# PLE operands as fp16 pairs split in the w_o stage, and DMA transposes for the last projection's x

## The chip, the cores and the metric

The kernel runs on one core of a Trainium2 chip. The metric is the device time of one execution in microseconds (us); lower is better. Engines are named as in the profile: PE (TensorE matmul), DVE (VectorE), ACT (ScalarE), POOL (GpSimd), SP (SyncE). "Full speed" of PE is its 2.4 GHz level, "half speed" its 1.2 GHz level.

## What is computed

One decoder layer on x of 1024 tokens by 1024 features, float32 in and out. Of the reference, cut to what matters here:

```
y  = sigmoid(gate_A) * (A @ W_A) + sigmoid(gate_B) * (Bm @ W_B);  x += y @ W_o
x += hierarchical MoE(RMSNorm(x))        # top-1 of 4 groups, then top-2 of 4 experts inside it
x += sigmoid(RMSNorm(x) @ W_pg) * (p @ W_ple)
```

p has 1024 tokens by 256 features, so `p @ W_ple` is a product of depth 256 (two slices of 128) and width 1024, called PLE below. `RMSNorm(x) @ W_pg` is the last projection: depth 1024, width 1024.

## The kernel before, in words

The tokens are cut in 8 tiles of 128. Products of float32 values are mostly done as three fp16 products: each operand is split into a high and a low fp16 part (`split`: ACT writes the high part, DVE the low part), and hi\*hi, lo\*hi and hi\*lo are summed in float32 in PSUM.

The program runs in stages:

- attention, convolution, gates and their merge, up to about 609 us;
- the **w_o stage**, about 609 to 697 us: for each token tile 48 matmuls of `out_proj`, then `norm2`, which writes fp16 high and low rows (`h2s`) and turns them by one DMA transpose on the SP queue (L682) for the router's small matmuls (`router_rows`, L688 and L690). The eight loads of x (L636) and the loads of `W_ple` (`wpl`) and of most of p transposed (`pTs`) go through the same SP queue;
- a **window**, about 697 to 724 us, in an order written out by hand on PE, ACT, DVE and POOL: the last third of the routing and the PLE products of token tiles 0 to 3, whose results are stored to memory. The routing ends in the table of token indices (`toki`, L985) from which POOL gathers the experts' rows (`xg`, `xtail`, L1010);
- 16 experts, about 720 to 964 us, whose weights arrive as 96 loads of 512 KB on the SP queue;
- six late PLE half tiles (`ple_late`), then a branch for overflow that all engines pass together (`tc.If`, L1254), and behind it the **final stage**, to the end: two more PLE half tiles, and for each token tile t its last projection.

In the final stage `combine` (with `mix`) gathers two rows per token by indirect DMAs from POOL (`yg`, L1239, four buffers) and adds them to `x2` on DVE (L1241); `turn` transposes x on PE (eight float32 transposes, L156, by `transpose_split`) and splits the result out of PSUM on ACT (L110) and DVE (L111); `final` does two half tiles of 24 matmuls (L1328 to L1330), and after each ACT applies the sigmoid (L1331), which frees the PSUM bank (there are two), and DVE multiplies by PLE and adds x (L1332, L1333). Each half tile's matmuls read the turned x of their own token tile. The PE order of the final stage is the order of the code; there `turn(t+1)` stands between the two halves of `final(t)`. ACT, DVE, POOL and SP are ordered by a scheduler.

`ple_mm` is the PLE product of one half tile: two float32 matmuls (the profile shows each as two rows of L889). A half tile in the final stage is evacuated by ACT in `ple_late` (L1234), one of the early ones in `evac` (L946).

Of the kernel before, what the change touches and what calls it, by code (L numbers as in the profile page):

```python
# [9 lines left out]
F32 = mybir.dt.float32  # L10
F32R = mybir.dt.float32r
BF = mybir.dt.bfloat16
FP16 = mybir.dt.float16
I32 = mybir.dt.int32
AF = mybir.ActivationFunctionType
# [4 lines left out]
S = 1024  # L20
D = 1024
NT = 8
# [12 lines left out]
NPL = 3  # L35
NPW = 4
# [11 lines left out]
XS = 16.0  # L48
# [3 lines left out]
HS = 256.0  # L52
PS = XS * HS
# [9 lines left out]
def trunk_layer(ctx: ExitStack, tc: tile.TileContext, x, wq0, wq, wc, wgb, wga, wA, wB, wo, wr,  # L63
                we, wpg, wple, pT, vecs, gains, out):
    nc = tc.nc
    def f(ap):
        return ap.bitcast(F32)

    def pool(stack, name, bufs=1, **kw):
        return stack.enter_context(tc.tile_pool(name=name, bufs=bufs, reuse_waits="tile", **kw))  # L70
# [37 lines left out]
    def split(hi, lo, src, lo_eng=None, scale=None):  # L108
        if scale is not None:
            nc.scalar.activation(hi, src, AF.Copy, scale=scale)  # L110
            nc.vector.scalar_tensor_tensor(lo, src, scale, hi, op0=ALU.mult, op1=ALU.subtract)  # L111
            return
        nc.scalar.activation(hi, src, AF.Copy)
        (lo_eng or nc.vector).tensor_tensor(lo, src, f(hi), op=ALU.subtract)
# [9 lines left out]
    def acc_bank():  # L124
        return bank("acc", 2)

    def tr_bank():
        return bank("tr", 2)
# [23 lines left out]
    def transpose_split(src, hi, lo, scale=None):  # L152
        for g in range(2):
            tr = tr_bank()
            for c in range(4):
                nc.tensor.transpose(tr[:, c * 128:(c + 1) * 128],  # L156
                                    src[:, (4 * g + c) * 128:(4 * g + c + 1) * 128], identF)
            t3 = tr.rearrange("p (c t) -> p c t", c=4)
            split(hi[:, 4 * g:4 * g + 4], lo[:, 4 * g:4 * g + 4], t3, scale=scale)
# [389 lines left out]
    def feat_mm(wp, h):  # L549
        acc = acc_bank()  # L550
        for k in range(8):
            mm3(acc, wp[0][:, k], wp[1][:, k], hTh[:, k, h * 512:(h + 1) * 512],
                hTl[:, k, h * 512:(h + 1) * 512], k, 8)
        return acc

    wBp = None
    for j in range(8):
# [4 lines left out]
        for h in range(2):  # L562
            hs = slice(h * 512, (h + 1) * 512)
            a = feat_mm(wb, h) if j else conv["b", h]
# [20 lines left out]
    wp_ = pool(mstack, "wo")  # L585
# [47 lines left out]
    x2 = xp.tile([128, NT, D], F32, name="x2")  # L633
# [1 line left out]
    for t in range(NT):  # L635
        nc.sync.dma_start(x2[:, t], x[t * 128:(t + 1) * 128, :])  # L636
    plep = pool(ctx, "ple", side="right")
    wpl = plep.tile([128, 2, D], F32, name="wpl")
    gp = pool(ctx, "route", side="right")
    rt = pool(ctx, "rt", side="right")  # L640
    pstack = ExitStack()
    plp0 = pool(pstack, "ple0", side="right")
    pTs = [pl_.tile([128, 2, n * 128], F32, name=f"pT{n}") for n, pl_ in ((NPL, plp0), (NT - NPL, plep))]
    fstack = ExitStack()
    fp = pool(fstack, "fw", side="right")
    gF = fp.tile([128, D], F32, name="gF")
# [14 lines left out]
    def out_proj(t, h, mid=None):  # L661
        tok = slice(t * 128, (t + 1) * 128)
        hs = slice(h * 512, (h + 1) * 512)
        a = acc_bank()
        for k in range(8):
            if k == 5 and mid:
                mid()
            wh, wl = wos[k]
            nc.tensor.matmul(a, lhsT=mTh[:, k, tok], rhs=wh[:, hs], start=k == 0, stop=False)
            nc.tensor.matmul(a, lhsT=mTl[:, k, tok], rhs=wh[:, hs], start=False, stop=False)  # L670
            nc.tensor.matmul(a, lhsT=mTh[:, k, tok], rhs=wl[:, hs], start=False, stop=k == 7)
        nc.vector.scalar_tensor_tensor(x2[:, t, hs], a, 1.0 / PS, x2[:, t, hs], op0=ALU.mult, op1=ALU.add)
# [12 lines left out]
    def router_rows(t, hT2):  # L685
        rb = o_bank()
        for k in range(8):
            nc.tensor.matmul(rb[:, :40], lhsT=hT2[:, 0, k], rhs=wrp[:, k].rearrange("p a e -> p (a e)"), start=k == 0,  # L688
                             stop=False)
            nc.tensor.matmul(rb[:, :20], lhsT=hT2[:, 1, k], rhs=wrp[:, k, 0], start=False, stop=k == 7)  # L690
        sm = fp.tile([128, 20], F32, name="sm", bufs=2)
        nc.vector.tensor_reduce(sm, rb[:, :40].rearrange("p (w e) -> p e w", e=20), axis=AX.X, op=ALU.add)
        nc.vector.scalar_tensor_tensor(lg[:, t], sm, 1.0 / PS, vt[:, 14:34], op0=ALU.mult, op1=ALU.add)
# [176 lines left out]
    for t in range(NT - 1):  # L870
        out_proj(t, 0)
        out_proj(t, 1)
        if t:
            router_rows(t - 1, hT2)
        hT2 = norm2(t)
        if t == 4:
            nc.sync.dma_start(wpl, wple)
            nc.sync.dma_start(pTs[0], pT[:, :, :NPL * 128])
            nc.sync.dma_start(pTs[1], pT[:, :, NPL * 128:])
        if t in CUTS[1:3]:  # L880
            i = CUTS.index(t)
            for _ in route(CUTS[i - 1], t, tb):
                pass

    def ple_mm(t, h, get=acc_bank):
        a = get()
        pTt, i = (pTs[0], t) if t < NPL else (pTs[1], t - NPL)
        for k in range(2):
            nc.tensor.matmul(a, lhsT=pTt[:, k, i * 128:(i + 1) * 128],  # L889
                             rhs=wpl[:, k, h * 512:(h + 1) * 512], start=k == 0, stop=k == 1)  # L890
        return a

    def ple_out(t, po):
        nc.scalar.dma_start(pl_d[t * 128:(t + 1) * 128, :], po)
# [37 lines left out]
    def ring_tile(name, i):  # L932
        return ring[0].tile([128, 1024], F32 if i == 1 else FP16, name=name, bufs=ring[i])
# [9 lines left out]
    po = [ring_tile("wraw", 1) for _ in range(NPW)]  # L943

    def evac(t, h, a):
        nc.scalar.activation(po[t][:, h * 512:(h + 1) * 512], a, AF.Copy)  # L946
        if h:
            ple_out(t, po[t])

# [21 lines left out]
    def w0_lo(i):  # L971
        gate_lo(w0[i])

    def ple_at(t, h, get):
        if t < NPL:
            evac(t, h, ple_mm(t, h, get))
# [14 lines left out]
    w0_lo(1)  # L991
    evac(3, 0, ple_mm(3, 0, s_bank))
    w0_lo(2)
    pstack.close()
    xstack = ExitStack()
    xq = pool(xstack, "moe", side="right")
    NB = (4, 2)
# [144 lines left out]
    for e, seq in enumerate(FIRST):  # L1142
        with tc.issue_after(mark.ins):
            halves, acts, nx = {}, [], None
            xT = xTs.pop(e)
            for c in seq:
                if c in "ABCD":
                    i = "ABCD".index(c)
# [3 lines left out]
                elif c == "h":  # L1152
                    we_, i = next(his)
                    gate_hi(allw[we_], we_src(we_))
                elif c == "l":
                    we_, i = next(lows)
# [14 lines left out]
    for e in range(e0, E - 1):  # L1171
# [3 lines left out]
        with ExitStack() as held:  # L1175
            if e < 3:
                held.enter_context(tc.issue_after(mark.ins))
            if e < E:
# [12 lines left out]
                xT, nx = xTs.pop(e), None  # L1191
# [20 lines left out]
    xT = xTs.pop(E - 1)  # L1212
# [3 lines left out]
    for c in LAST:  # L1216
        if c in "ABCD":
            i = "ABCD".index(c)
            halves[c] = expert_half(C, xT, ws, i // 2, i % 2)
        elif c == "k":  # L1220
            k = len(wps)
# [7 lines left out]
    pos = [ring_tile("wraw", 1) for _ in range(NPW, NT)]  # L1229

    def ple_late(i, get):
        t, h = NPW + i // 2, i % 2
        a = ple_mm(t, h, get)
        nc.scalar.activation(pos[t - NPW][:, h * 512:(h + 1) * 512], a, AF.Copy)  # L1234

    def mix(t, tile_):
        for c in range(2):
# [16 lines left out]
    with tc.If(ov > 0):  # L1254
# [12 lines left out]
        with tc.For_i(JB * E, 8 * E, E) as jb:  # L1267
            with tc.For_i(0, E) as ev:
# [6 lines left out]
                xT = expert_t(128, tl, xg)  # L1275
# [23 lines left out]
    ip = pool(ctx, "fin", side="right")  # L1299
# [11 lines left out]
        return plt  # L1311

    def turn(t):
        xh = ip.tile([128, 8, 128], FP16, name="xh", bufs=2)
        xl = ip.tile([128, 8, 128], FP16, name="xl", bufs=2)
        transpose_split(x2[:, t], xh, xl, 1.0)
        return xh, xl, row_norm(ip, x2[:, t], None, None, grow=HS)

    def final(t, plt, xh, xl, rs, mid):
        tok = slice(t * 128, (t + 1) * 128)  # L1320
        ot = ip.tile([128, D], F32, name="ot", bufs=3)
        edges = (0, 512, 1024) if t < NT - 1 else (0, 512, 768, 1024)
        for lo, hi in zip(edges, edges[1:]):
            hs = slice(lo, hi)
            a = acc_bank()[:, 0:hi - lo]
            for k in range(8):
                wh, wl = wps[k]
                nc.tensor.matmul(a, lhsT=xh[:, k], rhs=wh[:, hs], start=k == 0, stop=False)  # L1328
                nc.tensor.matmul(a, lhsT=xl[:, k], rhs=wh[:, hs], start=False, stop=False)  # L1329
                nc.tensor.matmul(a, lhsT=xh[:, k], rhs=wl[:, hs], start=False, stop=k == 7)  # L1330
            nc.scalar.activation(ot[:, hs], a, AF.Sigmoid, scale=rs)  # L1331
            V_.tensor_tensor(ot[:, hs], ot[:, hs], plt[:, hs], op=ALU.mult)  # L1332
            V_.tensor_tensor(ot[:, hs], ot[:, hs], x2[:, t, hs], op=ALU.add)  # L1333
            if t == NT - 1:
                nc.sync.dma_start(out[0, tok, hs], ot[:, hs])
            if lo == 0:
                nx = mid()
        if t < NT - 1:
            nc.scalar.dma_start(out[0, tok, :], ot)
        return nx  # L1340

    order.enter_context(tc.manual_schedule(engines={ET.PE}))
    with tc.high_priority():
        plts = [combine(0), combine(1)]
    for i in range(NQ, NR):
        ple_late(i, s_bank)
    with tc.high_priority():
        hs_ = turn(0)
    for i in range(NR, 2 * (NT - NPW)):
        ple_late(i, s_bank)  # L1350
    for t in range(NT):
        if t + 2 < NT:
            plts.append(combine(t + 2))
        hs_ = final(t, plts[t], *hs_, lambda: turn(t + 1) if t + 1 < NT else None)
    order.close()


# [77 lines left out]
```

## Time and profile before

| | before |
|---|---|
| median of 3 runs | 1088.74 us (1088.43 to 1091.41) |
| the profiled execution's own time | 1087.68 us |
| its span, first to last instruction | 1085.9 us |
| mean granted PE clock | 0.987 of full |
| busy PE / DVE / ACT / POOL | 1027.3 / 667.1 / 525.9 / 230.6 us |

The profiled execution takes 1.78 us more than its span, and stands 1.06 us below the median. Busy time of PE is read with care, since matmuls overlap: back to back, 128x512 fp16 matmuls start 0.2155 us apart although each row shows 0.38 us. The start times in the timeline give the pace. In the timelines the brackets hold the idle time ahead of an instruction and what ended it; queue entries that issue DMAs are marked SPq or ACTq.

### The profile page before, as it was taken

The numbers are of one execution on the slowest core, as the hardware profiler recorded it, in microseconds if no ns is written. First come the engines' busy times: TensorE is split into PE (matmuls) and PEld (weight loads), VectorE is DVE, ScalarE is ACT, GpSimd is POOL, SyncE is SP. The second block draws the span as 40 slices with busy tenths as digits, with TensorE's granted clock in tenths as the row PEclk, the third lists the DMA queues.
The fourth block names the chain that finished last, engine by engine and source line by source line (L and its number), as shares of the span: only waits on it lengthen the run. The fifth ranks groups of instructions, "written<-read, shape, count | busy, mean of one in ns | idle before, by whom it ended". The sixth has DMA issues, their size and how long they took to land. (4 is left out here: it accounts for less than half of the span.)

```text
span 1085.9 us, 17914 instructions
## 1 busy us (share of the span) xinstructions
PE 1027.3 (95%) x6664; PEld 589.9 (54%) x6664; DVE 667.1 (61%) x1430; ACT 525.9 (48%) x974; POOL 230.6 (21%) x343
## 2 busy tenths in 40 slices
PE   6898999999999999999998999887989999998898
PEld 4554555555555555444443444456767777744444
DVE  6778566676586572223248536748977888755643
ACT  6554455565555552212126322237767777553232
POOL 3552234223222100000015300231111110015300
PEclk9999999999999999999999999989999999998999
DMA  8257677568566763423448653399998999536501
GB/s 304 57 121 172 133 156 183 126 124 182 154 126 142 187 134 80 158 97 97 155 161 296 246 153 78 88 322 389 389 357 304 328 334 306 175 97 213 194 39 59
DMA packets 167117, 201.33 MB, mean 185 GB/s; under 512 B 122674, under 2 KB 126394, under 8 KB 166898
## 3 DMA queue, kind: packets, MB, share of 16 engines
q1 hardware_dynamic: 142898, 121.09, 39.9%
q0 software_dynamic: 15008, 53.29, 15.8%
q10 hardware_dynamic: 9120, 25.78, 6.5%
q8 instruction: 53, 0.87, 0.3%
q14 instruction: 38, 0.31, 0.1%
HBM read 138.69 MB, written 32.59 MB: 158 GB/s over the span
## 5 line engine op out<-in xcount | busy, mean ns | idle before, releaser
L117 PE MATMUL acc<-hTh,fwh 128*128 128x512 f16 x336 | 127.3, 379 | 1.3 <-DVE fg L419 1.1
L119 PE MATMUL acc<-hTh,fwl 128*128 128x512 f16 x336 | 127.3, 379 | 0.0
L118 PE MATMUL acc<-hTl,fwh 128*128 128x512 f16 x336 | 127.3, 379 | 0.0
L966 DVE SCALAR_TENSOR_TENSOR wl<-wraw,wh 128x1024 f16<-128x1024 f32 x64 | 77.9, 1220 | 22.6 <-ACT wh L961 21.7
L111 DVE SCALAR_TENSOR_TENSOR wl<-wraw,wh 128x1024 f16<-128x1024 f32 x47 | 57.9, 1245 | 51.0 <-ACT wh L110 48.9
L228 PE MATMUL acc<-wqh,hTh 128*128 128x384 f16 (+1 forms) x248 | 82.1, 331 | 5.1 <-ACT hTh L110 4.5
L229 PE MATMUL acc<-wqh,hTl 128*128 128x384 f16 (+1 forms) x248 | 82.3, 332 | 2.5 <-DVE hTl L111 2.5
L230 PE MATMUL acc<-wql,hTh 128*128 128x384 f16 (+1 forms) x248 | 82.4, 332 | 0.0
L314 ACT ACTIVATE P<-P,st 128x128 f32<-128x128 f32 (+3 forms) x64 | 49.5, 773 | 66.5 <-DVE st L311 51.1
L961 ACT ACTIVATE wh<-wraw 128x1024 f16<-128x1024 f32 x64 | 67.0, 1054 | 18.8 <-PE acc L1046 11.8
L110 ACT ACTIVATE wh<-wraw 128x1024 f16<-128x1024 f32 x47 | 49.1, 1055 | 54.2 <-PE acc L118 26.4
L323 DVE SCALAR_TENSOR_TENSOR hl<-P,st,hl 128x128 f16<-128x128 f32 (+3 forms) x64 | 52.7, 839 | 23.6 <-ACT hl L322 23.2
L306 DVE CUSTOM_DVE_ANT_0 P<-s,base 128x512 f32<-128x512 f32 (+2 forms) x96 | 51.6, 553 | 14.7 <-PE s L305 11.1
L1046 PEld LDWEIGHTS <-wh 128*128 128x128 f16 x512 | 50.5, 99 | 7.0 <-issue 3.4
L322 ACT ACTIVATE hl<-P,st 128x128 f16<-128x128 f32 (+3 forms) x64 | 46.7, 768 | 15.3 <-DMA pTr<-hl 8.6
L119 PEld LDWEIGHTS <-fwl 128*128 128x128 f16 x336 | 32.9, 98 | 37.8
L1329 PE MATMUL acc<-wh,xl 128*128 128x512 f16 (+1 forms) x136 | 50.2, 369 | 3.1 <-DVE xl L111 3.1
L1045 PEld LDWEIGHTS <-wh 128*128 128x128 f16 x512 | 51.1, 100 | 1.8
L118 PEld LDWEIGHTS <-fwh 128*128 128x128 f16 x336 | 32.9, 98 | 35.2 <-issue 1.7
L117 PEld LDWEIGHTS <-fwh 128*128 128x128 f16 x336 | 32.9, 98 | 34.2
L1328 PE MATMUL acc<-wh,xh 128*128 128x512 f16 (+1 forms) x136 | 50.4, 370 | 0.0
L1330 PE MATMUL acc<-wl,xh 128*128 128x512 f16 (+1 forms) x136 | 50.1, 368 | 0.0
(328 smaller groups left out, 2537.0 us busy)
## 6 DMA issues: line engine op xcount, KB each, us to landing
wraw<-in_we_dram SPq DMA_DIRECT2D x96, 512.0 KB
Yd<-yt ACTq DMA_DIRECT2D x14, 512.0 KB
fraw<-in_wc_dram POOLq DMA_DIRECT2D x12, 512.0 KB, 5.7
wraw<-in_wq_dram POOLq DMA_DIRECT2D x24, 192.0 KB, 4.0
P<-in_x_dram SPq DMA_DIRECT2D x8, 512.0 KB
fraw<-in_wga_dram POOLq DMA_DIRECT2D x8, 512.0 KB, 4.6
base<-brow POOLq DMA_DIRECT2D x8, 512.0 KB, 3.6
sga<-fg POOLq DMA_DIRECT2D x8, 512.0 KB, 3.4
```

What stands on the lines that cost most here:

```text
L111: nc.vector.scalar_tensor_tensor(lo, src, scale, hi, op0=ALU.mult, op1=ALU.subtract)
L117: nc.tensor.matmul(acc, lhsT=whi, rhs=xhi, start=k == 0, stop=False)
L118: nc.tensor.matmul(acc, lhsT=whi, rhs=xlo, start=False, stop=False)
L119: nc.tensor.matmul(acc, lhsT=wlo, rhs=xhi, start=False, stop=k == nk - 1)
L228: nc.tensor.matmul(acc[:, :w], lhsT=hTh[:, k, tok], rhs=wh[:, :w], start=k == 0, stop=False)
L229: nc.tensor.matmul(acc[:, :w], lhsT=hTl[:, k, tok], rhs=wh[:, :w], start=False, stop=False)
L230: nc.tensor.matmul(acc[:, :w], lhsT=hTh[:, k, tok], rhs=wl[:, :w], start=False, stop=k == 7)
L306: nc.vector.tensor_tensor_reduce(out=pt[:, c0:c0 + valid], in0=sb[:, :valid], in1=base[:, c0:c0 + valid], scale=1.0, scalar=-3e38, op0=ALU ...
L323: nc.vector.scalar_tensor_tensor(hl[:, :qt + 1, 1], p3, r, hl[:, :qt + 1, 0], op0=ALU.mult, op1=ALU.subtract)
L961: nc.scalar.activation(wh, raw, AF.Copy, scale=HS)
L966: V_.scalar_tensor_tensor(wl, raw, HS, wh, op0=ALU.mult, op1=ALU.subtract)
L1045: nc.tensor.matmul(a[:, :n], lhsT=wh[:, k], rhs=xT[:, k, 0, :n], start=k == 0, stop=False)
```

## The change

`W_ple` and p transposed are no longer loaded as float32 tiles. In the first four turns of the w_o stage's loop one 512 KB slice each (two of `wple`, then two of `pT`) is loaded through the single `woraw` buffer and split into fp16 pairs, and `ple_mm` does six fp16 matmuls in place of two float32 ones; the evacuations take the scale out. In the final stage tiles 0 and 1 are turned on PE as before, but both ahead of the last two PLE half tiles; tiles 2 to 7 are split in rows (token-major) into one `rows` buffer, and turned by a DMA transpose on the SP queue. `turn(t+2)` stands between the halves of `final(t)`. The turned x has three buffers, `ot` two.

```diff
-    wpl = plep.tile([128, 2, D], F32, name="wpl")
+    wpl = [plep.tile([128, 2, D], FP16, name=f"wpl{i}") for i in range(2)]
+    pTs = [plep.tile([128, 2, S], FP16, name=f"pT{i}") for i in range(2)]
...
-        if t == 4:
-            nc.sync.dma_start(wpl, wple)
-            nc.sync.dma_start(pTs[0], pT[:, :, :NPL * 128])
-            nc.sync.dma_start(pTs[1], pT[:, :, NPL * 128:])
+        if t < 4:
+            k = t % 2
+            dst, src, sc = ((wpl, wple, HS), (pTs, pT, XS))[t // 2]
+            raw = wp_.tile([128, D], F32, name="woraw", bufs=1)
+            nc.sync.dma_start(raw, src[:, k, :])
+            split(dst[0][:, k], dst[1][:, k], raw, scale=sc)
...
     def ple_mm(t, h, get=acc_bank):
         a = get()
-        pTt, i = (pTs[0], t) if t < NPL else (pTs[1], t - NPL)
+        tok, hs = slice(t * 128, (t + 1) * 128), slice(h * 512, (h + 1) * 512)
         for k in range(2):
-            nc.tensor.matmul(a, lhsT=pTt[:, k, i * 128:(i + 1) * 128],
-                             rhs=wpl[:, k, h * 512:(h + 1) * 512], start=k == 0, stop=k == 1)
+            nc.tensor.matmul(a, lhsT=pTs[0][:, k, tok], rhs=wpl[0][:, k, hs], start=k == 0, stop=False)
+            nc.tensor.matmul(a, lhsT=pTs[0][:, k, tok], rhs=wpl[1][:, k, hs], start=False, stop=False)
+            nc.tensor.matmul(a, lhsT=pTs[1][:, k, tok], rhs=wpl[0][:, k, hs], start=False, stop=k == 1)
         return a
...
     def turn(t):
-        xh = ip.tile([128, 8, 128], FP16, name="xh", bufs=2)
-        xl = ip.tile([128, 8, 128], FP16, name="xl", bufs=2)
-        transpose_split(x2[:, t], xh, xl, 1.0)
+        xT = ip.tile([128, 2, 8, 128], FP16, name="xT", bufs=3)
+        xh, xl = xT[:, 0], xT[:, 1]
+        if t < 2:
+            transpose_split(x2[:, t], xh, xl, 1.0)
+        else:
+            rows = ip.tile([128, 2, D], FP16, name="rows", bufs=1)
+            split(rows[:, 0], rows[:, 1], x2[:, t], scale=1.0)
+            nc.sync.dma_start_transpose(xT.rearrange("p a k t -> p (a k) t"), rows.rearrange("p a d -> p (a d)"))
         return xh, xl, row_norm(ip, x2[:, t], None, None, grow=HS)
...
-        ot = ip.tile([128, D], F32, name="ot", bufs=3)
+        ot = ip.tile([128, D], F32, name="ot", bufs=2)
...
-        hs_ = turn(0)
+        hs_ = [turn(0), turn(1)]
     for i in range(NR, 2 * (NT - NPW)):
         ple_late(i, s_bank)
     for t in range(NT):
         if t + 2 < NT:
             plts.append(combine(t + 2))
-        hs_ = final(t, plts[t], *hs_, lambda: turn(t + 1) if t + 1 < NT else None)
+        hs_ = [hs_[1], final(t, plts[t], *hs_[0], lambda: turn(t + 2) if t + 2 < NT else None)]
```

The change moves instructions in three places. First PE behind the branch (`tr<-identF,x` are the turns, `s<-wpl,pT` the last two PLE half tiles, `acc<-wh,xh` the last projection). Before:

```order
L1254 UNCONDITIONAL_BRANCH x2
L156 MATMUL tr<-identF,x_6008 128x128 x8
L889 MATMUL s<-wpl,pT_6032 128x512 x4
L1328 LDWEIGHTS xh
L1328 MATMUL acc<-wh,xh 128x512
L1329 LDWEIGHTS xl
L1329 MATMUL acc<-wh,xl 128x512
```

Now:

```order
L1254 UNCONDITIONAL_BRANCH x2
L156 MATMUL tr<-identF,x_6008 128x128 x16
L889 LDWEIGHTS pT_6023
L889 MATMUL s<-wpl_6021,pT_6023 128x512
L890 LDWEIGHTS pT_6023
L890 MATMUL s<-wpl_6022,pT_6023 128x512
L891 LDWEIGHTS pT_6024
L891 MATMUL s<-wpl_6021,pT_6024 128x512
```

The transposes of tile 1 now stand ahead of the PLE half tiles and of the whole of tile 0's projection; before they stood between its halves. Twelve PLE matmuls follow, then the last projection without any further transpose.

Second, ACT in the final stage (`s,rn_ss<-x` are the squares of the row norm, `xh<-tr` or `xT<-tr` the high parts of a turn on PE, `rows<-x` the high parts of a turn by DMA, `ot<-acc` the sigmoids, `wraw<-s` the PLE evacuations). Before:

```order
L140 ACTIVATE s,rn_ss<-x_6008 128x512 x2
L110 ACTIVATE xh<-tr 128x512 x2
L1234 ACTIVATE wraw<-s 128x512 x2
L140 ACTIVATE s,rn_ss<-x_6008 128x512 x2
L1331 ACTIVATE ot<-acc,rn_ss 128x512
L110 ACTIVATE xh<-tr 128x512 x2
L1331 ACTIVATE ot<-acc,rn_ss 128x512
L140 ACTIVATE s,rn_ss<-x_6008 128x512 x2
L1339 DMA out_dram<-ot 128x1024
L1331 ACTIVATE ot<-acc,rn_ss 128x512
```

Now, from the squares of tile 1:

```order
L140 ACTIVATE s,rn_ss<-x_6008 128x512 x2
L110 ACTIVATE xT<-tr 128x512 x2
L1234 ACTIVATE wraw<-s 128x512
L110 ACTIVATE rows<-x_6008 128x1024
L1234 ACTIVATE wraw<-s 128x512
L1336 ACTIVATE ot<-acc,rn_ss 128x512
L110 ACTIVATE rows<-x_6008 128x1024
L1336 ACTIVATE ot<-acc,rn_ss 128x512
L140 ACTIVATE s,rn_ss<-x_6008 128x512 x2
L110 ACTIVATE rows<-x_6008 128x1024
L1344 DMA out_dram<-ot 128x1024
L1336 ACTIVATE ot<-acc,rn_ss 128x512 x2
```

The row splits of tiles 2, 3 and 4 stand between the sigmoids of tile 0 and ahead of those of tile 1; each but the first waits until the transpose of the tile before has left the one `rows` buffer.

Third, the SP queue at the start of the w_o stage (`x` are the eight loads of x, `hT<-h2s` the DMA transposes of `norm2`). Before:

```order
L602 DMA g<-cgb 128x1024
L636 DMA x_6008<-in_x_dram 128x1024 x8
L877 DMA wpl<-in_wple_dram 128x2048
L879 DMA pT_6032<-in_pT_dram 128x2x640
L682 DMA_TRANSPOSE hT_6151<-h2s 128x16x128
L682 DMA_TRANSPOSE hT_6239<-h2s 128x16x128
```

Now:

```order
L602 DMA g<-cgb 128x1024
L636 DMA x_6008<-in_x_dram 128x1024 x8
L878 DMA woraw<-in_wple_dram 128x1024
L680 DMA_TRANSPOSE hT_6149<-h2s 128x16x128
L878 DMA woraw<-in_pT_dram 128x1024 x2
L680 DMA_TRANSPOSE hT_6241<-h2s 128x16x128
```

One of the four slices is loaded ahead of x; two now stand between the first and the second DMA transpose of `norm2`, and each waits until the split before it has read `woraw`.

## Rows read from the trace of the kernel before

**Rows 1.** Page, busy time by engine: busy us, share of the span, instructions.

```profile
PE 1027.3 (95%) x6664; PEld 589.9 (54%) x6664; DVE 667.1 (61%) x1430; ACT 525.9 (48%) x974; POOL 230.6 (21%) x343
```

**Rows 2.** Waits of PE, 960 to 1086 us, for a split: total, times, longest.

```profile
PE acc L1329 <- DVE xl L111: 3.1, 1, 3.1
```

**Rows 3.** Timeline of PE, late PLE and final stage: start, us, what, [idle before].

```profile
964.25 3.60 PE L889 MATMUL acc<-wpl,pT 128*128 128x512 f32 x8
967.68 3.60 PE L889 MATMUL tr<-wpl,pT 128*128 128x512 f32 x8
...
978.21 1.37 PE L156 MATMUL tr<-identF,x 128*128 128x128 f32 x8 [3.50 <-DVEq L1254]
979.38 5.02 PE L889 MATMUL s<-wpl,pT 128*128 128x512 f32 x8
984.23 0.38 PE L1328 MATMUL acc<-wh,xh 128*128 128x512 f16 x1
984.45 0.38 PE L1329 MATMUL acc<-wh,xl 128*128 128x512 f16 x1
...
992.32 1.82 PE L156 MATMUL tr<-identF,x 128*128 128x128 f32 x8 [2.74 <-DVE x L1241]
993.92 0.63 PE L1328 MATMUL acc<-wh,xh 128*128 128x512 f16 x1
...
995.63 0.51 PE L1329 MATMUL acc<-wh,xl 128*128 128x512 f16 x1
...
1005.26 1.04 PE L156 MATMUL tr<-identF,x 128*128 128x128 f32 x8
1006.13 0.38 PE L1328 MATMUL acc<-wh,xh 128*128 128x512 f16 x1
```

**Rows 4.** Timeline of DVE, final stage: gathered rows of tile 1 are added.

```profile
990.88 1.28 DVE L1241 SCALAR_TENSOR_TENSOR x<-yg,gate_m,x 128x1024 f32<-128x1024 f32 x1 [1.19 <-DMA yg<-Yd,loci]
```

**Rows 5.** Timeline of POOL, behind the branch.

```profile
980.03 0.58 POOL L1310 DMA_DIRECT2D plt<-pld  x1 [7.91 <-DMA Yd<-xg]
983.92 0.99 POOL L1239 DMA_INDIRECT yg<-Yd,loci  x1 [3.31 <-ACT wraw L1234]
```

**Rows 6.** Timeline of PE and of DVE in the window, and PE's stall behind it.

```profile
703.35 6.57 PE L889 MATMUL acc<-wpl,pT 128*128 128x512 f32 x8
...
730.82 0.58 PE L1025 MATMUL tr<-identH,xtail 128*128 128x128 f16 x4 [3.23 <-DMA xtail<-h2d,toki]
...
710.02 0.23 DVE L830 TENSOR_TENSOR G<-s,OH 128x64 f32<-128x64 f32 x1 [2.21 <-PE s L825]
...
712.74 0.19 DVE L985 CAST toki<-s 128x32 int32<-128x32 f32 x1 [0.27 <-PE s L779]
```

**Rows 7.** Busy time by stretch: PE, PEld, DVE, ACT, POOL, PE clock, DMA share, GB/s.

```profile
735.00:860.00 125.00, 112.48 (x1196) 87.85 (x1194) 103.97 (x166) 91.26 (x134) 19.49 (x32) 0.99 0.98 356
...
614.00:628.00 14.00, 14.00 (x66) 6.37 (x65) 4.81 (x7) 3.23 (x7) 0.57 (x1) 1.00 1.02 413
...
684.40:688.40 4.00, 4.00 (x24) 1.86 (x22) 2.04 (x4) 1.07 (x3) 0.55 (x1) 1.00 0.93 169
...
1000.00:1020.00 20.00, 16.88 (x84) 8.11 (x82) 15.23 (x18) 5.71 (x13) 9.57 (x9) 1.00 0.69 248
```

**Rows 8.** Line L682, the DMA transposes of the w_o stage: ns min/median/max on the queue.

```profile
L682 SPq DMA_TRANSPOSE hT<-h2s x7: 3810/3937/4300, 625.4 to 692.4; - x7
```

**Rows 9.** Timelines, one such transpose: its last source on DVE, and PE waiting.

```profile
683.01 1.22 DVE L679 TENSOR_TENSOR h2s<-h,h2s 128x1024 f16<-128x1024 f32 x1
...
690.43 0.19 PE L688 MATMUL o<-wrp,hT 128*128 128x40 f16 x1 [1.59 <-DMA hT<-h2s]
```

**Rows 10.** Page, the splits of 128x1024: DVE's low part, ACT's high part.

```profile
L111 DVE SCALAR_TENSOR_TENSOR wl<-wraw,wh 128x1024 f16<-128x1024 f32 x47 | 57.9, 1245 | 51.0 <-ACT wh L110 48.9
...
L110 ACT ACTIVATE wh<-wraw 128x1024 f16<-128x1024 f32 x47 | 49.1, 1055 | 54.2 <-PE acc L118 26.4
```

**Rows 11.** Tile yg, the gathers: us from issue to landing, min/median/max.

```profile
DMA to landing us min/median/max: 5.5/5.9/7.3
```

More of the change, by code (lines that the diff above doesn't have):

```diff
@@ L637, in trunk_layer @@
     plep = pool(ctx, "ple", side="right")
-    wpl = plep.tile([128, 2, D], F32, name="wpl")
+    wpl = [plep.tile([128, 2, D], FP16, name=f"wpl{i}") for i in range(2)]
+    pTs = [plep.tile([128, 2, S], FP16, name=f"pT{i}") for i in range(2)]
     gp = pool(ctx, "route", side="right")
     rt = pool(ctx, "rt", side="right")
-    pstack = ExitStack()
-    plp0 = pool(pstack, "ple0", side="right")
-    pTs = [pl_.tile([128, 2, n * 128], F32, name=f"pT{n}") for n, pl_ in ((NPL, plp0), (NT - NPL, plep))]
     fstack = ExitStack()
@@ L945, in evac @@
     def evac(t, h, a):
-        nc.scalar.activation(po[t][:, h * 512:(h + 1) * 512], a, AF.Copy)
+        nc.scalar.activation(po[t][:, h * 512:(h + 1) * 512], a, AF.Copy, scale=1.0 / PS)
         if h:
@@ L993, in trunk_layer @@
     w0_lo(2)
-    pstack.close()
     xstack = ExitStack()
@@ L1233, in ple_late @@
         a = ple_mm(t, h, get)
-        nc.scalar.activation(pos[t - NPW][:, h * 512:(h + 1) * 512], a, AF.Copy)
+        nc.scalar.activation(pos[t - NPW][:, h * 512:(h + 1) * 512], a, AF.Copy, scale=1.0 / PS)
     def mix(t, tile_):
```

## The prediction
> **What bounds the kernel now.** I read the page's busy times first, then PE's timeline and waits by stage, then the engines that PE waits for. PE is busy 95% of the span [rows 1], so it is the bound nearly everywhere, and a shorter product is worth its time only where PE doesn't wait afterwards for something that comes no earlier. That question is asked at each place where the change saves PE time. In PE's timeline of the last stages [rows 3] the reader is to see three pieces of idle time: 3.50 us ahead of the first turn (all engines pass the branch together, behind the adds of tile 0's gathers), 2.74 us ahead of the second turn (x of tile 1), and 3.1 us in the middle of a projection for a late split [rows 2]. The middle one is decisive: the last gathered rows of tile 1 are added from 990.88 to 992.16 [rows 4], and the turn of tile 1 starts right then, at 992.32. This moment is set by POOL's gathers, whose first behind the branch starts at 983.92 after 3.31 us without work [rows 5], and by 5.5 to 7.3 us from issue to landing [rows 11]. Nothing in the change moves it.
>
> **PLE, 16 half tiles.** Eight rows of float32 PLE, which are two half tiles, take 967.68 - 964.25 = 3.43 us at full speed, 1.72 us each [rows 3]. Six fp16 matmuls at 0.2155 us (984.23 to 984.45 in the same rows, averaged over a half tile) are 1.29 us. That is 0.42 us saved in each, 6.8 us of PE time in all. Where it counts:
>
> - Six late half tiles, 964 to 975 us: 2.5 us saved, counted **0**. PE runs idle into the branch behind them, until 978.21, for DVE's adds of tile 0, which wait for gathers. If that cover were gone, PE would gain at most these 2.5 us.
> - Eight early half tiles in the window. The first two take 6.57 us, against 3.43 at full speed, so they run at half speed [rows 6]. The routing's small matmuls are queued behind them on PE, and DVE, in turn, waits 2.21 us for these, at 710.02. From there the chain goes on to the token table at 712.74, the experts' gathers and their first matmuls. Twelve fp16 matmuls at half pace (four in 1.71 us from 993.92 to 995.63 [rows 3], so 0.43 each) take 5.1 us, so the chain comes about 1.3 us earlier, at most 2.2 (DVE's whole wait) and at least 0.4, should only the pace of later work change. I take **-1.2**. The experts behind it have idle time on PE early on (112.48 us busy of 125 [rows 7]), mostly on chains of DVE and ACT behind the weights; the later experts leave none. I let the gain pass through.
> - The last two half tiles are part of the final stage below.
>
> The order of the experts' gathers also changes on POOL: the tail rows of the second pair move ahead of two full gathers. PE waits 3.23 us for them at 730.82 [rows 6]. But the first weight split on ACT waits for its load there as well, so I count 0, and keep the 3.2 us as a rival's gain. Reordered splits in the first experts: 0, within 2 us either way, by the size of PE's idle pieces there.
>
> **The w_o stage.** Four loads of 512 KB replace three larger ones, and four splits are added: 1.05 us on ACT and 1.25 on DVE each [rows 10], which have room: PE is the only busy engine there (14.00 of 14.00 us, DVE 4.81, ACT 3.23 [rows 7]). What can cost is the order on SP: both pT slices are queued ahead of the second DMA transpose, each waiting for the split before it; and on ACT the first pT split stands ahead of the second token tile's high part. At 413 GB/s [rows 7] a slice moves in 1.3 us; behind the first transpose (3.9 us on the queue [rows 8]) I get the two slices landed at about 632 and 638, the second transpose issued near 636, hence landed near 642, and its reader on PE due near 643 (157 matmuls of 0.2155 us into the stage). I take **+0.3**; from 0 to +2.5, if both loads come late.
>
> **The final stage.** This part is counted along PE. Now the turn of tile 1 stands ahead of the last PLE half tiles and of everything of tile 0. PE does turn 0 as before, to 979.6, and then waits for x of tile 1 until 992.3: 12.7 us instead of working from 979.38 to 989.4. Then the turn runs to 993.92 as before; twelve PLE matmuls, four at half pace and eight at full, take 3.5 us, to 997.4. Tile 0's first half takes 24 x 0.2155 = 5.17, so its second half starts at 1002.57 instead of 993.92: **+8.65**. Given back are six turns of 1006.13 - 1005.26 = 0.87 us [rows 3], **-5.2**; the wait for the late split [rows 2], **-3.1**, since x of tile 2 no longer goes through PSUM; and the four matmuls at half pace that came behind the turn (0.86), **-0.9**, now counted in the PLE. That makes -0.55. After 12.7 us idle PE may stay at half speed longer than after 2.74: **+0.4**, from 0 to +1.4.
>
> Last, a new chain. A DMA transpose takes 3.9 us on its queue [rows 8], and from the end of its last source (683.01 + 1.22) to the reader's start at 690.43 it is 6.2 us [rows 9], all wait. With one `rows` buffer, the high part of tile t+1 on ACT waits for the landing of tile t. On this path: rows of tile 2 ready on DVE near 1000.3, landed 1006.5; rows of tile 3 at 1009.2 behind DVE's adds, landed 1015.4; the high part of tile 4 then takes 1.05 us on ACT, with an output DMA behind it, and only then comes tile 1's first sigmoid, done near 1017.6. It frees the bank that tile 2's projection needs at 1018.1, when PE ends tile 1. The margin is 0.5 us, and two transposes lie in series, so each us more in both costs 2 us on PE. Gathers and transposes share the DMA engines, at a share of 0.69 already [rows 7]. I take **+2**, one us and a quarter more per transpose, between 0 (the price of rows 9) and +5 (2.75 us more each). Later tiles have a margin of 2 us, without gathers.
>
> On the transposes the trace says 169 GB/s while one was under way against 413 GB/s for plain loads [rows 7]. The Trainium skill (Advanced Engine Details and Errata, section DMA Advanced Topics, X-Bar Transpose) says that transposes are as fast as plain DMAs on this chip, 350 to 400 GB/s. By that rule the 512 KB would take some 1.4 us (an estimate from that page), 2.5 less than the 3.9 of rows 8, in each of two; the margin would be about 5 us, and the +2 would be 0. I go by the rows.
>
> **Sum.** +0.3 - 1.2 - 0.55 + 0.4 + 2 = +0.95. The execution shown took 1087.68, which gives 1088.6; the median stands 1.06 higher, so the forecast is **1089.7**. Within 0.3%, or 3.3 us, is about what a measurement of this kernel can't tell from no change: 1085.5 to 1092.0.
>
> **Rivals.**
>
> - *Slower: the one rows buffer.* ACT is in order, so a late landing of tile 3 holds tile 1's sigmoids, these hold the two banks, and PE stands. It decides from about 2.4 us more per transpose than in rows 9: 2 x 2.4 - 0.5 is a wait of 4.3, which takes the sum past 1092. At 3.4 us more the wait is 6.3 in place of 2: **1094**. For it: gathers under way at 1000 to 1013. Against: gathers end soon after. Chance 0.28.
> - *Faster: the early wait shrinks.* If POOL's 3.31 us ahead of the first gather [rows 5] belong to something that the new order moves, x of tile 1 comes 3 us earlier, and PE with it; or the 3.23 us stall in the window goes by the new gather order. Either gives 1089.7 - 3.2, and with no new wait -2 more: **1084.5**. Against: the profile names an ACT evacuation as releaser of the first, but all engines met at the branch after it. Chance 0.2.
> - *Transposes at the pace of plain loads*, as a mechanism: two transposes in series 2 us quicker, no wait for banks: **1087.7**. Against: rows 7 to 9. Chance 0.12.
>
> **How the numbers follow.** Forecast 0.40. It and the third rival lie within 0.3%: 0.52. Faster 0.20, slower 0.28. The forecast's own range, from its bounds, is 1086 to 1093; the range reaches into both rivals, 1084.0 to 1094.3, leaving 1 in 10 on each side.
>
> **What would show it.** In the profile after: PLE rows of 0.2155 us pitch; routing on DVE about 1 us earlier than 710.02; PE idle about 12 us behind the first turn, ending within 0.5 us of the add for tile 1; no transposes on PE afterwards; tile 0's second half from about 1002.6; the transposes on SP at 4 us, landing 6 to 8 us after their rows; and PE waiting for a sigmoid of tile 1 ahead of tile 2. I am wrong if PE has that idle piece shorter by 3 us or more, if it then runs without any wait to the end (third rival), or if it waits for banks more than 5 us.

## The result and the profile after

| | before | after |
|---|---|---|
| median | 1088.74 us (1087.22 to 1091.41, 5 runs) | 1096.08 us (1092.09 to 1099.13, 5 runs) |
| ratio, 95% interval | | 1.0061 [1.0038, 1.0085] |
| the profiled execution / its span | 1087.68 / 1085.9 us | 1099.13 / 1097.4 us |

The change made the kernel slower, by 4 to 9 us in this measurement. The forecast was 1089.7 with a range to 1094.3. A second measurement of the unaltered change (below) gave a median of 1093.4 over 12 runs, ratio 1.0040 [1.0017, 1.0063], which is 2 to 7 us. The profiled execution after is the slowest of its five, and its span is 11.5 us longer than that of before. I therefore read it by stages, beside the profile of the second measurement ("change again"), and put down to the change only what both show.

| stage, by its first instruction to the next one's | before | after | change again |
|---|---|---|---|
| first load of x (L636) to token table `toki` | 101.86 | 103.86 | 100.88 |
| token table to the first late PLE matmul | 251.51 | 254.08 | 251.61 |
| late PLE to the first turn | 13.96 | 13.54 | 13.64 |
| final stage: first turn to the end of the span | 107.7 | 113.0 | 114.9 |

Only the final stage is clearly longer in both profiles of the change, by 5.3 and 7.2 us. The other 6 us of the first profile lie in stages where the second is no longer than before to within 0.1 us; no run explains them. In the final stage PE loses time although over the whole span it is busy 5 us less than before [rows 1]:

```profile
PE 1022.3 (93%) x6648; PEld 586.2 (53%) x6648; DVE 670.0 (61%) x1428; ACT 529.9 (48%) x972; POOL 231.9 (21%) x343
```

What PE waits for from 980 us to the end, after: total, times, longest:

```profile
PE tr L156 <- DVE x L1241: 11.8, 1, 11.8
PE tr L156 <- DVEq L1254: 5.0, 1, 5.0
PE acc L1333 <- ACT ot L1336: 4.8, 2, 3.1
```

The wait for the late split [rows 2] is gone, and one for the sigmoids (`ot`) has come. PE's timeline after, which answers to [rows 3]: start, duration, what, [idle before]:

```profile
984.38 1.94 PE L156 MATMUL tr<-identF,x 128*128 128x128 f32 x8 [5.03 <-DVEq L1254]
998.14 1.94 PE L156 MATMUL tr<-identF,x 128*128 128x128 f32 x8 [11.82 <-DVE x L1241]
999.87 0.63 PE L889 MATMUL s<-wpl,pT 128*128 128x512 f16 x1
1000.30 0.63 PE L890 MATMUL s<-wpl,pT 128*128 128x512 f16 x1
...
1008.28 0.38 PE L1333 MATMUL acc<-wh,xT 128*128 128x512 f16 x1
...
1020.46 0.38 PE L1333 MATMUL acc<-wh,xT 128*128 128x512 f16 x1 [1.65 <-ACT ot L1336]
...
1028.94 0.58 PE L1333 MATMUL acc<-wh,xT 128*128 128x512 f16 x1 [3.14 <-ACT ot L1336]
1029.32 0.63 PE L1334 MATMUL acc<-wh,xT 128*128 128x512 f16 x1
1029.74 0.63 PE L1335 MATMUL acc<-wl,xT 128*128 128x512 f16 x1
```

Behind the first turn there is one idle piece of nearly 12 us. Two new ones start at 1018.8 and 1025.8. Behind the second of these PE starts matmuls at a pitch of 0.43 us, which is half speed (the granted clock is 0.50 from 1028.9 to 1031.9). ACT's rows say what held the sigmoids:

```profile
1003.42 1.06 ACT L110 ACTIVATE rows<-x 128x1024 f16<-128x1024 f32 x1 [0.81 <-DVE x L1241]
...
1008.54 0.69 ACT L1336 ACTIVATE ot<-acc,rn_ss 128x512 f32<-128x512 f32 x1 [3.58 <-PE acc L1335]
1018.77 1.06 ACT L110 ACTIVATE rows<-x 128x1024 f16<-128x1024 f32 x1 [9.54 <-DMA xT<-rows]
1019.74 0.67 ACT L1336 ACTIVATE ot<-acc,rn_ss 128x512 f32<-128x512 f32 x1
...
1026.47 1.06 ACT L110 ACTIVATE rows<-x 128x1024 f16<-128x1024 f32 x1 [4.70 <-DMA xT<-rows]
```

The high part of tile 3 stood 9.54 us for the transpose of tile 2 to leave `rows`. The second sigmoid of tile 0 was queued behind it, and PE stood for the bank that this sigmoid frees. The high part of tile 4 then held the sigmoids of tile 1 in the same way. In the chain of waits the transpose of tile 2 is one piece, from its issue to its landing:

```profile
1005.81 12.86 DMA xT<-rows
```

Before, in the w_o stage, a transpose of the same 512 KB took 6.2 us to its reader [rows 9]. It was not alone there: a plain store of 512 KB, issued by ACT, ran beside it.

```profile
684.27 0.33 ACTq L680 DMA_DIRECT2D h2d<-h2s  x1
```

Here, beside gathers, it took 12.9 us, and the gathers stood as well. DVE's adds of gathered rows after:

```profile
1009.42 1.28 DVE L1241 SCALAR_TENSOR_TENSOR x<-yg,gate_m,x 128x1024 f32<-128x1024 f32 x1 [1.26 <-DMA yg<-Yd,loci]
1017.90 1.28 DVE L1241 SCALAR_TENSOR_TENSOR x<-yg,gate_m,x 128x1024 f32<-128x1024 f32 x1 [7.20 <-DMA yg<-Yd,loci]
```

Busy time by stretch, up to about that landing (columns as in [rows 7]):

```profile
1011.80:1013.80 2.00, 2.00 (x11) 0.92 (x10) 0.00 (x0) 0.00 (x0) 0.11 (x1) 1.00 0.96 169
1013.80:1015.80 2.00, 2.00 (x11) 0.88 (x9) 0.00 (x0) 0.00 (x0) 0.00 (x0) 1.00 1.24 114
1015.80:1017.80 2.00, 2.00 (x11) 0.90 (x10) 0.00 (x0) 0.00 (x0) 0.00 (x0) 1.00 1.06 388
```

The DMA engines read as fully busy, at 114 and 169 GB/s; from 1015.8 they move 388. A full share with less than half of the bytes is the sign to look for. It stood in the trace of before already: a share of 0.93 at 169 GB/s from 684.4 to 688.4 [rows 7].

The DMA view says how long the packets of each queue held the engines: packets, MB, share of the time of all 16 engines. For the SP queue after, first from 1005 to 1020 us (the transpose of tile 2, beside gathers), then from 1029 to 1070 (the last four transposes, behind the gathers and beside stores of the output):

```profile
q1 hardware_dynamic: 2080, 0.52, 37.6%
```

```profile
q1 hardware_dynamic: 8320, 2.10, 29.9%
```

So, as the profile counts it, the packets of one transpose held all the engines for 5.6 us beside gathers, and for 3.1 us without. In the w_o stage before, beside the plain store, it was 3.7 us (46.0% from 683.5 to 691.5).

### The profile page after: what moved, and what is told of

The parts are those of the page before. It is cut to its first block, busy times and chain, and to the rows that moved or that the text cites. A ratio compares the mean times of both kernels' runs of the same rounds, so it can differ in the third digit from the quotient of the medians.

```text
span 1097.4 us, 17905 instructions
## 1 busy us (share of the span) xinstructions
PE 1022.3 (93%) x6648; PEld 586.2 (53%) x6648; DVE 670.0 (61%) x1428; ACT 529.9 (48%) x972; POOL 231.9 (21%) x343
## 2 busy tenths in 40 slices
DMA packets 179485, 204.48 MB, mean 186 GB/s; under 512 B 135170, under 2 KB 138634, under 8 KB 179394
## 5 line engine op out<-in xcount | busy, mean ns | idle before, releaser
L967 DVE SCALAR_TENSOR_TENSOR wl<-wraw,wh 128x1024 f16<-128x1024 f32 x64 | 77.7, 1218 | 25.4 <-ACT wh L962 25.4
L111 DVE SCALAR_TENSOR_TENSOR wl<-wraw,wh 128x1024 f16<-128x1024 f32 x47 | 58.0, 1244 | 49.4 <-ACT wh L110 47.8
L1333 PE MATMUL acc<-wh,xT 128*128 128x512 f16 (+1 forms) x136 | 50.5, 371 | 4.8 <-ACT ot L1336 4.8
L1334 PE MATMUL acc<-wh,xT 128*128 128x512 f16 (+1 forms) x136 | 50.3, 370 | 0.0
L1335 PE MATMUL acc<-wl,xT 128*128 128x512 f16 (+1 forms) x136 | 50.3, 370 | 0.0
```

Of the source, the lines that this page charges most:

```text
L967: V_.scalar_tensor_tensor(wl, raw, HS, wh, op0=ALU.mult, op1=ALU.subtract)
```

## The experiments

Each ratio is against runs of the kernel before, measured along with the experiment. "Final stage" is, as above, from the first turn to the end of the span, in one profile of each kernel.

**The PLE half alone.** The final stage is put back to that of before (two `xh`, `xl` buffers, `turn(t+1)` on PE between the halves, three `ot`); only the fp16 PLE stays.

```diff
-        hs_ = [turn(0), turn(1)]
+        hs_ = turn(0)
...
-        hs_ = [hs_[1], final(t, plts[t], *hs_[0], lambda: turn(t + 2) if t + 2 < NT else None)]
+        hs_ = final(t, plts[t], *hs_, lambda: turn(t + 1) if t + 1 < NT else None)
```

> Only the PLE half of the change (fp16 pairs, split in the w_o stage); the final stage is that of before. Theory A (the lasting loss lies in the final stage alone; what the trace after shows as 5 us lost in one expert near 800 us belongs to that execution): the window gains about 1.2 us and the last two PLE half tiles about 1.5, so about 1086 us, faster than before by 2 to 3. Theory B (the PLE half itself costs, through the reordered splits of the experts or the later router transposes): about 1091 to 1093, slower than before by 2 to 5, with a PE wait of 3 us or more for the output scaling of one expert and half speed behind it.

Measured: 1084.22 us (1080.66 to 1090.58), ratio 0.9968 [0.9947, 0.9989]; final stage 105.4. So this half gains, between 1 and 6 us, and the loss is not in it: theory A for the time. Theory A's remark on one expert did not hold, since the wait of 3.5 us is in this profile too (see "The experts" below).

**The final stage's half alone.** The float32 PLE and its three loads are put back.

```diff
-        if t < 4:
...
-            split(dst[0][:, k], dst[1][:, k], raw, scale=sc)
+        if t == 4:
+            nc.sync.dma_start(wpl, wple)
...
-            nc.tensor.matmul(a, lhsT=pTs[1][:, k, tok], rhs=wpl[0][:, k, hs], start=False, stop=k == 1)
+            nc.tensor.matmul(a, lhsT=pTt[:, k, i * 128:(i + 1) * 128],
+                             rhs=wpl[:, k, h * 512:(h + 1) * 512], start=k == 0, stop=k == 1)
```

> Only the final stage's half of the change (two turns on PE first, DMA transposes of rows from tile 2), PLE in float32 as before. Theory A: from the first turn behind the branch to the end 5 us longer than before's 107.7, that is about 113, and the whole about 1094; transposes of tiles 2 and 3 land 10 us or more after issue. Theory B: the final stage alone costs little in the median: about 1089 to 1090.

Measured: 1098.43 us (1097.78 to 1100.63), ratio 1.0108 [1.0086, 1.0130]; final stage 117.1. The loss is all here. PE's waits in the final stage:

```profile
PE tr L156 <- DVE x L1241: 12.4, 1, 12.4
PE acc L1333 <- ACT ot L1336: 6.9, 1, 6.9
```

and ACT behind tile 2's transpose, which was issued at 1002.14 and so took 17.7 us:

```profile
1019.88 1.06 ACT L110 ACTIVATE rows<-x 128x1024 f16<-128x1024 f32 x1 [14.78 <-DMA xT<-rows]
```

**The order of the turns undone, the transposes kept.** `turn(1)` goes back between the halves of `final(0)`; tiles 2 to 7 still go by DMA.

```diff
-        hs_ = [turn(0), turn(1)]
+        hs_ = [turn(0)]
...
+    def mid(t):
+        if t == 0:
+            hs_.append(turn(1))
+        if t + 2 < NT:
+            hs_.append(turn(t + 2))
...
+        final(t, plts[t], *hs_[t], lambda: mid(t))
```

> The change with PE's order of the first turns undone: tile 1 is turned on PE between the halves of tile 0's projection, as before; tiles 2 to 7 by DMA still. If the 12 us idle piece ahead of tile 1 is what costs, 8.65 us of PE work move into it and the whole is about 1088. If the transposes that lie beside the gathers set the pace (landing 12.9 us after issue for tile 2), tile 2's projection is reached earlier and only waits longer for them, and the whole stays above 1092.

Measured: 1083.62 us (1078.04 to 1087.02), ratio 0.9957 [0.9939, 0.9974]; final stage 101.8. The time is below both figures expected. PE's waits in the final stage:

```profile
PE acc L1333 <- DMA xT<-rows: 2.1, 1, 2.1
PE tr L156 <- DVE x L1241: 2.0, 1, 2.0
```

The transpose of tile 2 is still slow (9.8 us), but PE has a half tile of tile 0 and all of tile 1 left to do by then, and pays 2.1 us of wait and 1.7 us at half speed (eight matmuls at 0.43). Both theories had priced a slow transpose higher here than it came. PE's two turns, and the start of the second half of tile 0:

```profile
980.88 1.94 PE L156 MATMUL tr<-identF,x 128*128 128x128 f32 x8 [5.61 <-DVEq L1254]
...
994.71 1.07 PE L156 MATMUL tr<-identF,x 128*128 128x128 f32 x8 [2.00 <-DVE x L1241]
995.61 0.38 PE L1333 MATMUL acc<-wh,xT 128*128 128x512 f16 x1
```

**As the last, with transposes only from tile 5.** Tiles 1 to 4 are turned on PE between the halves. Against the change:

```diff
-        if t < 2:
+        if t < 5:
...
+    def mid(t):
+        if t + 1 < 5:
+            hs_.append(turn(t + 1))
+        if 5 <= t + 2 < NT:
+            hs_.append(turn(t + 2))
```

> As the kernel e4_turn_order, but tiles 1 to 4 are turned on PE between the halves as before, and only tiles 5 to 7 by DMA, when the gathers are over. Theory A: no bank wait on PE, transposes land 5 to 6 us after issue; the final stage is before's less three turns of 0.87 us and about 1.5 us of PLE, so about 103.5 us, and the whole about 1083 to 1085. Theory B: the experts' loss stays, about 1088 to 1090.

Measured: 1080.96 us (1077.33 to 1084.43), ratio 0.9947 [0.9928, 0.9966]; final stage 101.4. It beats both kernels. From the run above it isn't separated, since the intervals overlap. The transposes now start at 1020.1, behind the last gathers, with stores of the output going on, and every one whose landing could be matched landed 4.6 us after its issue:

```profile
L1321 SPq DMA_TRANSPOSE xT<-rows x3: 1814/1917/2060, 1020.1 to 1041.7; - x3
...
DMA to landing us min/median/max: 4.6/4.6/4.6
```

**The same with transposes from tile 4** (`5` becomes `4` in the three places).

> As the kernel e5_dma_from_5, with tile 4 by DMA as well. If tile 4's transpose starts after the last gather has landed, one more PE turn goes: final stage 101.4 - 0.87 = 100.5 us, about 1080. If it lies beside the last gathers, it lands after 9 us or more, PE waits for it 1 to 3 us, and the gain is gone: 101 to 103.

Measured: 1082.92 us (1078.33 to 1085.78), ratio 0.9945 [0.9927, 0.9964]; final stage 103.7. No gain over tile 5, but not for the reason expected: PE waits for no transpose, and 3.26 us for a split out of PSUM on DVE (L111), which neither expectation had.

**The change's order, transposes only from tile 5.** This takes the slow transposes away and leaves the order of PE.

```diff
-        if t < 2:
+        if t < 5:
```

> PE's order of the change kept (turns 0 and 1 first), but tiles 2 to 4 turned on PE and only 5 to 7 by DMA, so that no transpose lies beside the gathers. Theory C (two causes add up: PE's order costs 8.65 us, and transposes beside gathers cost 4.8 us of bank waits and 1.4 us at half speed behind them): the final stage, 113.0 us with the change, becomes 113.0 - 6.2 + 3 x 0.87 = 109.4, transposes land under 5 us, no bank wait. Theory D (the order alone, the waits being its consequence): the waits stay or move to the splits, 113 to 115 us.

Measured: 1088.19 us (1084.88 to 1092.26), ratio 1.0007 [0.9989, 1.0025]; final stage 110.5. The idle piece of 12 us is there, the waits for sigmoids are not, and the gathers land at most 5.6 us after their issue. So each cause is there without the other: the order here, the slow transposes in the run with the order undone. They don't simply add. By the final stages, with 0.87 us for each of the three turns that go from PE, early transposes cost 3.0 us where the order is undone (101.8 against 101.4) and 5.1 and 7.0 us where it is kept (113.0 and 114.9 against 110.5). The order of the turns alone costs 9.1 us (110.5 against 101.4).

**The change once more**, unaltered.

> The change unaltered, again. Theory C: final stage 112 to 115 us from the first turn behind the branch, a transpose of tile 2 that lands 10 us or more after issue, the expert wait of 3.5 us again; the whole about 1092 to 1096 us, 4 to 7 above before.

Measured: 1093.4 us (1086.83 to 1098.09), ratio 1.0040 [1.0017, 1.0063]; final stage 114.9. Both causes come again. PE's waits in the final stage:

```profile
PE tr L156 <- DVE x L1241: 11.8, 1, 11.8
PE acc L1333 <- ACT ot L1336: 5.4, 2, 3.7
```

and on ACT tile 3's high part, standing until 1014.08 for a transpose that was issued at 998.08, 16.0 us:

```profile
1014.08 1.06 ACT L110 ACTIVATE rows<-x 128x1024 f16<-128x1024 f32 x1 [11.56 <-DMA xT<-rows]
```

**Plain copies in place of the transposes.** Same bytes, buffers, queue and order.

```diff
-            nc.sync.dma_start_transpose(xT.rearrange("p a k t -> p (a k) t"), rows.rearrange("p a d -> p (a d)"))
+            nc.sync.dma_start(xT.rearrange("p a k t -> p (a k t)"), rows.rearrange("p a d -> p (a d)"))
```

> The change with each DMA transpose replaced by a plain DMA copy of the same bytes between the same buffers, with the same waits; this leaves out turning tiles 2 to 7. If it is the way a transpose moves its bytes that suffers beside gathers (theory C), the copy of tile 2 lands within 6 us, bank waits on PE vanish, and the final stage is about 106.8 us (113.0 less 6.2). If it is the bytes, the single rows buffer or the order on ACT (rival), the copy of tile 2 also lands after 9 us or more and PE waits for a sigmoid 4 us or more: about 112 us.

Measured: 1086.19 us (1082.2 to 1095.84), ratio 0.9990 [0.9966, 1.0014]; final stage 106.6, PE waits for no sigmoid. The copy of tile 2, issued at 997.65, had landed by 1004.69, 7.0 us:

```profile
1004.69 1.06 ACT L110 ACTIVATE rows<-x 128x1024 f16<-128x1024 f32 x1 [3.76 <-DMA xT<-rows]
```

That is 1 us later than expected, and nowhere near the 9 us of the rival. So one `rows` buffer and the order of ACT cost PE no wait while a move takes 7 us. But a transpose also has more packets than a copy: 179485 in the change, 167869 here. After this run I took that for the reason.

**Copies in small pieces**, to test this.

```diff
-            nc.sync.dma_start_transpose(xT.rearrange("p a k t -> p (a k) t"), rows.rearrange("p a d -> p (a d)"))
+            xv = xT.rearrange("p a k t -> p (a k) t")
+            for i in range(2):
+                nc.sync.dma_start(xv[:, i::2], rows[:, i].rearrange("p (k t) -> p k t", t=128))
```

> Each DMA transpose of the change becomes two plain DMA copies, one for the high and one for the low rows, whose destination lies in pieces of 256 bytes (eight per partition and half, every other one), so that the same 512 KB of tiles 2 to 7 move in about as many small packets as a transpose has (2048 pieces against about 2061 packets more per transpose). The turning of tiles 2 to 7 is left out. If it is the number of small packets that slows transposes and gathers beside each other: as in the change, a copy of tile 2 that lands 10 us or more after its issue, gathers that land after 10 us or more, 4 to 5 us of waits of PE for tile 0's or 1's sigmoids, a final stage of 112 to 115 us and a median near 1093. If it is the turning itself: as with the whole copies, landed within 7 to 8 us, no wait of PE for a sigmoid, gathers within 7.5 us, a final stage of 106 to 108 us and a median near 1086.

Measured: 1085.64 us (1081.75 to 1091.62), ratio 0.9982 [0.9962, 1.0002]; final stage 107.4, no wait of PE for a sigmoid. The packets are those of the change to within two, and their bytes to 0.01 MB. The copies of tile 2, from 997.53, had landed by 1005.61, 8.1 us. The pages' packet rows, first of the change, then of this kernel:

```profile
DMA packets 179485, 204.48 MB, mean 186 GB/s; under 512 B 135170, under 2 KB 138634, under 8 KB 179394
```

```profile
DMA packets 179487, 204.49 MB, mean 189 GB/s; under 512 B 135171, under 2 KB 138635, under 8 KB 179395
```

The gathers' landing (tile `yg`) in this kernel, us from issue, least, median and most:

```profile
DMA to landing us min/median/max: 4.3/5.8/7.2
```

The same row in the change's second profile:

```profile
DMA to landing us min/median/max: 4.4/5.9/15.7
```

The number and size of the packets are not the reason, then; it is the turning itself. The DMA view adds to this. The SP queue's row for tile 2, first here from 997 to 1006.5 us, then in the change's second profile from 997.5 to 1015:

```profile
q1 hardware_dynamic: 2080, 0.52, 26.0%
```

```profile
q1 hardware_dynamic: 2080, 0.52, 50.0%
```

The two copies have as many packets as a transpose, and beside gathers they held the engines for 2.5 us, where the transpose took 5.6 us in the change's first profile and 8.8 in its second. Later copies in this kernel, behind the gathers, took 2.4 us for 512 KB. So the packets of these copies take the same time with gathers or without, while those of a transpose take 3.1 us without gathers and up to 8.8 beside them. Why they do can't be seen from here.

## Why the prediction was wrong

**The step that failed is the last term of the sum, +2 for the chain of transposes**, put there as "one us and a quarter more per transpose, between 0 and +5 (2.75 us more each)". Where 7.5 us were taken for tile 2's transpose, and at most 9, the change's two profiles show 12.9 and 16.0. PE's waits for banks were 4.8 and 5.4 us in place of 2. Half speed behind the longer wait cost another 1.4 us in the first profile (seven matmuls at 0.43 in place of 0.2155) and 1.7 in the second (eight), against +0.4 for half speed in all, which was meant for the idle piece behind the first turn. The price had the uncovered time of [rows 9] and a DMA share of 0.69 [rows 7] under it, and no row of a transpose beside gathers. From the row at 169 GB/s the forecast took the bytes and not the share of 0.93 beside them, and most of these bytes were the plain store's. Transposes and gathers hold each other up: some 60 to 210 GB/s at a share of 0.6 to 1.8 for most of that time, and a gather landed after as much as 15.7 us, where 7.3 was the longest before [rows 11].

Which rival it was: *the one rows buffer*, chance 0.28. Its chain is the one in ACT's rows above: late landing, sigmoids held, banks held, PE stands. It set in earlier than forecast: the first bank that PE stood for was that of tile 0's second sigmoid, and the forecast's chain begins with tile 1's first. Its condition was 2.4 us more on each of two transposes; there were 6.7 and 9.8 more on the first, and none on the second, which had landed 5.4 and 5.5 us after its rows. Its price, 6.3 us of wait, is close to what waits and half speed come to, 6.2 and 7.1; with the delay spread otherwise, that closeness is in part luck. Its "against", that gathers end soon after, was wrong, since the transpose itself delays them. It was named and priced, and should have had the larger chance.

The Trainium skill (Advanced Engine Details and Errata, DMA Advanced Topics, X-Bar Transpose) has transposes as fast as plain DMAs. Beside gathers the runs don't agree: in the same place, with the same bytes, a plain copy took 7.0 us and transposes 12.9 to 16.0.

**The terms that held.** The final stage by its other terms is 107.7 + 8.65 - 5.2 - 3.1 - 0.9 = 107.2 us. The kernel with plain copies took 106.6, the one with small pieces 107.4. So the four terms are right as a sum, to within 0.6 us in two kernels of one profile each. With the waits and the half speed above it comes to 113.4 and 114.3, where the change's two profiles show 113.0 and 114.9. One by one:

- *Order, +8.65*: PE idle for 11.82 us behind the first turn (12.7 forecast), until the add of tile 1. Tile 0's second half starts at 1008.28, which is 23.90 us behind the first turn; before it was 15.71, so it comes 8.2 us later. Undoing the order gives, from 107.7, minus 5.2, 3.1 and 0.9, minus 0.3 since the second turn starts that much sooner behind the first (13.83 us, 14.11 before), minus 0.7 since it is done in 0.90 and not 1.60 us, plus the 2.1 and 1.7 of that run: 101.3 against 101.8 measured.
- *Six turns, -5.2, and the late split, -3.1*: both gone from PE's rows.
- *The late PLE, 0*: late PLE to first turn shrank by 0.3 to 0.4 us, not 2.5; the idle time ahead of the branch grew from 3.50 to 5.03 us. The cover held.
- *The gathers' start*: POOL waits 3.23 us ahead of the first gather, 3.31 before [rows 5]. The faster rival's first reason, that this would move, did not come:

```profile
989.99 0.98 POOL L1239 DMA_INDIRECT yg<-Yd,loci  x1 [3.23 <-issue]
```

- *The w_o stage, +0.3*: PE waits 2.4 us there for the transposes of `norm2` in the first profile and 1.5 in the second, 1.6 before, within the bounds of 0 to +2.5.

The faster rival's second reason came without its gain. PE's stall of 3.23 us for `xtail` [rows 6] is gone, but in its place PE waits for `xg`, and longer for a copy on ACT (1.5 us before; in the second profile 3.8). PE's waits from 716 to 800 us after:

```profile
PE tr L1025 <- ACT xT L1030: 7.3, 1, 7.3
...
PE tr L1025 <- DMA xg<-h2d,toki: 1.8, 1, 1.8
```

**The window, -1.2.** The first PLE matmul to the row of DVE that waits for routing was 6.67 us before [rows 6], and is 5.41 now, 1.26 less:

```profile
708.63 0.59 PE L889 MATMUL acc<-wpl,pT 128*128 128x512 f16 x1
...
714.04 0.23 DVE L828 TENSOR_TENSOR G<-s,OH 128x64 f32<-128x64 f32 x1 [0.95 <-PE s L823]
```

That is the forecast, but in part by luck of the clock. With the float32 PLE of the second experiment the same piece took 5.14 us, since PE was granted half speed for part of it only (0.73 on average; 0.56 before, 0.50 in the change). With the fp16 PLE it took 4.55 to 5.41 us in nine profiles. Whether the gain reaches the end isn't shown by itself: in kernels of one profile each, the whole stretch from the loads of x to the token table runs from 99.66 to 103.86 us.

**The experts, "0, within 2".** One expert near 800 us takes 18.0 to 20.6 us in the profiles with the fp16 PLE, 15.6 in those without (from the transposes of its gathered rows, L1025, to those of the next expert). In the change DVE has two low weight splits (L967) ahead of the scaling (L1092) for which PE waits:

```profile
798.06 2.35 DVE L967 SCALAR_TENSOR_TENSOR wl<-wraw,wh 128x1024 f16<-128x1024 f32 x2
800.44 1.28 DVE L1092 SCALAR_TENSOR_TENSOR yt<-s,yt 48x512 f32<-48x512 f32 x2
...
801.18 0.61 PE L1087 MATMUL s<-wh,hq 128*128 128x512 f16 x1 [3.45 <-DVE yt L1092]
```

It comes back elsewhere: from the token table to the late PLE it is +2.6 us in one profile of the change and +0.1 in the other, and over all profiles 249.6 to 254.1 us with the fp16 PLE, 251.5 and 253.6 without. That the scheduler's new order of DVE makes this expert long is an association; no run undid it alone.

**Sum.** With the 4.8 and 1.4 measured in place of the +2.4 for transposes and half speed, the forecast would have been 1093.5. The second measurement's median is 1093.4, the first's 1096.1, so that the sum meets the second to 0.1 us is luck. The step above accounts for 3.8 us; what else the first median has over the forecast is not traced to any term.

## What to carry to other kernels

A DMA transpose that is quick beside plain stores must not be priced at that where indirect gathers run; either keep transposes behind the last gather, or turn those tiles on PE. Moving a late operand's work to the head of an in-order queue exposes the whole wait for the operand. By the sum that ate 8.65 of the 9.2 us given back here, and it cost 9.1 us between two kernels that differ only in the order of the turns. And one buffer with an in-order engine behind it turns a slow transfer into a stall of engines that don't read it at all.

## What was not expected of the hardware

A transpose of 512 KB and indirect gathers slow each other well past their sum of bytes. Beside gathers the transpose of tile 2 landed 9.8 to 17.7 us after its issue in four profiles; without gathers most transposes landed after 4.2 to 5.2 us, with stores of the output going on. In the three of these four profiles that have the change's order, the slowest gather landed after 12.2, 15.7 and 16.9 us. Plain copies with the same number of packets in the same place landed after 8.1 us, and the gathers beside them after 7.2 us at most. Whether a transpose also slows other kinds of loads was not tested. And identical programs vary: 12 runs of one kernel spread over 7 to 14 us, so that a gain of 3 us shows only in the medians of many.
